# One argument to the tile framework: the order of a decoder layer's instructions is laid down against its time-line model

## Chip, cores and metric

The kernel runs on one core of a Trainium2 chip. The metric is the device time of one execution in microseconds (us); the table further down gives the median of three runs.

## What is computed

One decoder layer for a prompt of 1024 tokens and eight sample sequences of 8 tokens each, which share all weights. The reference, cut to what matters:

```python
def decoder_layer(x, c, lp, attend, s0_re, s0_im):
    mod = jax.nn.silu(c) @ lp['ada_w'] + lp['ada_b']
    sh1, sc1, g1, sh2, sc2, g2, sh3, sc3, g3 = jnp.split(mod, ADA_CHUNKS, axis=-1)
    h = x + 0.5 * g1[:, None, :] * swiglu(rms_modulate(x, lp['norm_ffn1'], sh1, sc1),
                                          lp['ffn1_w_in'], lp['ffn1_w_out'])
    mix, k, v, sr, si = token_mixer(rms_modulate(h, lp['norm_mix'], sh2, sc2), lp, attend, s0_re, s0_im)
    h = h + g2[:, None, :] * mix
    h = h + 0.5 * g3[:, None, :] * swiglu(rms_modulate(h, lp['norm_ffn2'], sh3, sc3),
                                          lp['ffn2_w_in'], lp['ffn2_w_out'])
    return h, k, v, sr, si

def token_mixer(u, lp, attend, s0_re, s0_im):
    q, k, v, xs, ga, gb = jnp.split(u @ lp['w_in'], IN_SPLITS, axis=-1)
    o_a = attend(q, k, v, lp['sb_bias'])          # stick-breaking attention, 8 heads of 64
    y, sr, si = s5_ssm(xs, ...)                   # 32 groups, one complex state of 64 each
    zg = jax.nn.gelu(y)
    o_b = zg * jax.nn.sigmoid(zg @ lp['glu_w'] + lp['glu_b'])
    merged = jax.nn.sigmoid(ga) * (o_a @ lp['w_branch_a']) + jax.nn.sigmoid(gb) * (o_b @ lp['w_branch_b'])
    return merged @ lp['w_out'], k, v, sr, si
```

The width is 1024, the inner width of the two feed-forward nets 2816. All tensors are float32; the kernel multiplies in pairs of 16-bit parts (three products for one).

## The kernel before, in words

Activations lie transposed: 128 partitions by 8 slices of the model width, with 1092 columns (1024 prompt tokens, 64 sample tokens, 4 of padding), which are worked in three chunks of 364 or two halves of 546. The program is straight-line: Python loops are unrolled while it is traced, and there is no branch on the device.

Its stages follow each other: the first feed-forward net (`ffn`, up to 755 us of the profile), with the projection of the conditioning (`ada_steps`) and the tables of the state-space model (`ssm_params`, `ssm_prep`) traced into it; the combined input projection and the state-space run (`mixer_a`, `ssm_run`); the gated unit (`glu`); attention of prompt and samples with the rest of the projection as side work (`attend_prompt`, `attend_sample`, the list `gates`); the merge of the two branches and the output projection (`mixer_b`); the second `ffn`; the final norm.

Weights come through the class `Weights`: `fetch` issues a DMA on SyncE's queue into one of two buffers `wf` (L122), `measure` takes their largest magnitude on VectorE (L89), GpSimd spreads it over the partitions (L82), and `split` cuts them into two 16-bit parts, the high one on ScalarE (L101), the low one on VectorE (L102). In the feed-forward nets, `seven_products` (from L468) computes one block of 128 inner channels with seven products of 24 matmuls each, in three PSUM tiles X, Y and Z that are added to more than once. Its last VectorE reads are L503 (of Y, after the product `s3`), L506 and L510. Product `a22` writes to Y again, and so waits for L503:

```python
    add(Y, "s3", "t3", False)
    v.tensor_add(c22, view(Y), c22)
    tick()
    add(Z, "s4", "b22", False)
    ...
    add(Y, "a22", "t4", False)
```

Who sets the order: the kernel only traces instructions. When the block `tile.TileContext` closes, the framework's scheduler lays down one list for each engine and each DMA queue. It plays the program against a model of the machine. Each time an engine can take an instruction, it takes the one that was traced first among those that are ready at that moment of the model. On the chip each list then runs strictly in the order laid down, and an instruction whose input is late holds back all that stand behind it. By default the model is the framework's plain simulator; its choices are thus those of a moment that the plain simulator reckoned. Two kinds of edges bind the scheduler whatever the model is: `tc.issue_after(ins)` (the block's instructions on that engine stand behind `ins`) and `tc.keep_in_program_order`. Which buffer of a pool a tile gets is decided in the same pass.

## Time and profile before

| what | value |
|---|---|
| median of 3 runs | 2384.77 us |
| lowest, highest | 2381.21 us, 2393.02 us |
| the profiled execution's own time | 2397.24 us |
| its span, first to last instruction | 2395.5 us |
| TensorE busy | 2287.6 us (95%), 18391 matmuls |
| VectorE busy | 1678.2 us (70%) |
| ScalarE busy | 969.2 us (40%) |
| mean granted clock of TensorE | 0.982 of full |

The span is the time of all five engines together; busy is the time in which an engine had an instruction in work. TensorE's busy time is modelled at the ends of its matmuls, since they are pipelined. The granted clock is the share of full speed (2.4 GHz) at which TensorE could run; half of it is 1.2 GHz.

### The profile page before, as it was taken

What the parts mean: (1) busy time and instruction counts of PE and PEld (TensorE: products, weight loads), DVE (VectorE), ACT (ScalarE), POOL (GpSimd) and SP (SyncE); (2) the same over time, 40 slices, a digit from 0 to 9 for tenths busy, and PEclk for the clock granted to TensorE, in tenths of its full rate; (3) what the DMA queues carried; (4) which work ended last, traced back from release to release, by engine and by line L of the source; (5) the groups of instructions that cost most, each with busy time, mean ns of one, the idle gap of its engine ahead of it and who ended that gap; (6) DMA issues with size and microseconds to landing.
All of it is one profiled execution on the core that took longest, in us unless ns stands there. A gap on an engine that the chain in (4) does not pass through costs nothing.

```text
span 2395.5 us, 42875 instructions
## 1 busy us (share of the span) xinstructions
PE 2287.6 (95%) x18391; PEld 1626.9 (68%) x18391; DVE 1678.2 (70%) x3026; ACT 969.2 (40%) x1244; POOL 141.8 (6%) x193
## 2 busy tenths in 40 slices
PE   5999999999999999899999997999999999999997
PEld 2677778777787666685544452655688878888884
DVE  5966698886797626446788787697677655777735
ACT  3533331233331521245788787324443321333403
POOL 0000000000000000001133300000000000000000
PEclk8999999999999999989999998999999999999999
DMA  8133334433333144445244323522111143111302
GB/s 308 55 119 108 108 120 140 152 108 123 135 145 126 54 146 146 110 158 185 75 137 136 109 67 128 187 77 84 61 52 55 34 139 111 63 54 54 129 19 76
DMA packets 94191, 262.83 MB, mean 110 GB/s; under 512 B 13152, under 2 KB 50400, under 8 KB 83760
## 3 DMA queue, kind: packets, MB, share of 16 engines
q1 hardware_dynamic: 83632, 240.23, 29.3%
q0 software_dynamic: 5312, 17.34, 2.5%
q10 hardware_dynamic: 5056, 2.52, 0.5%
q8 instruction: 144, 2.36, 0.4%
q14 instruction: 47, 0.39, 0.1%
HBM read 204.10 MB, written 49.66 MB: 106 GB/s over the span
## 4 chain that ended last, share of the span: by engine, by line
PE 54%; DVE 13%; ACT 7%; DMA 5%; issue 3%; POOL 1%; SPq 1%; another core or an unknown queue 0%; ACTq 0%; DVEq 0%; POOLq 0%
PE u L481 19%; PE u L242 13%; PE u L226 11%; PE u L216 2%; PE z L1368 2%; DVE wl L102 2%; DVE mx L89 2%; DMA wf<-in_ffn_w_in 2%; ACT ae L1098 1%; DMA wf<-in_w_in 1%; PE z L226 1%; PE z L994 1%; PE o L1112 1%; DMA aw<-in_ada_w 1%; ACT ae L1016 1%
## 5 line engine op out<-in xcount | busy, mean ns | idle before, releaser
L226 PE MATMUL u<-u,wh 128*128 128x364 f16 (+1 forms) x1632 | 391.6, 319 | 6.3 <-ACT u L398 4.3
L242 PE MATMUL u<-h,wh 128*128 128x272 f16 (+1 forms) x2304 | 366.2, 280 | 4.9 <-DVE h L102 4.9
L101 ACT ACTIVATE wh<-wf,sc 128x1024 f16<-128x1024 f32 (+2 forms) x130 | 183.2, 1410 | 371.4 <-PE u L242 179.8
L89 DVE TENSOR_REDUCE mx<-wf 128x1 f32<-128x1024 f32 (+2 forms) x136 | 211.1, 1575 | 145.3 <-DMA wf<-in_ffn_w_in 80.3
L481 PE MATMUL u<-u,wh 128*128 128x272 f16 (+1 forms) x1824 | 288.0, 279 | 1.7 <-DVE mx L89 1.3
L242 PEld LDWEIGHTS <-wh 128*128 128x128 f16 x2560 | 249.2, 97 | 59.3 <-issue 6.9
L481 PEld LDWEIGHTS <-wh 128*128 128x128 f16 x2432 | 234.6, 98 | 66.3 <-issue 19.7
L226 PE MATMUL u<-u,wl 128*128 128x364 f16 (+1 forms) x816 | 260.2, 319 | 1.1 <-DVE wl L102 1.1
L102 DVE SCALAR_TENSOR_TENSOR wl<-wf,sc,wh 128x1024 f16<-128x1024 f32 (+2 forms) x130 | 209.2, 1609 | 73.3 <-ACT wh L101 72.8
L226 PEld LDWEIGHTS <-wh 128*128 128x128 f16 x1824 | 176.4, 98 | 114.7 <-issue 15.0
L242 PE MATMUL u<-h,wl 128*128 128x274 f16 (+1 forms) x1152 | 228.3, 280 | 0.0
L481 PEld LDWEIGHTS <-w3h 128*128 128x128 f16 x1824 | 175.7, 97 | 43.6 <-issue 7.4
L481 PE MATMUL u<-fac,w3h 128*128 128x272 f16 x1216 | 192.7, 279 | 0.0
L481 PE MATMUL u<-u,wl 128*128 128x272 f16 (+1 forms) x912 | 179.7, 278 | 0.0
L82 POOL PARTITION_ALL_REDUCE am<-mx x106 | 53.8, 514 | 1871.3 <-DVE mx L89 1834.1
L242 PEld LDWEIGHTS <-wl 128*128 128x128 f16 x1280 | 124.3, 97 | 26.9
L481 PEld LDWEIGHTS <-wl 128*128 128x128 f16 x1216 | 118.1, 97 | 26.2 <-issue 0.4
L226 PEld LDWEIGHTS <-wl 128*128 128x128 f16 x912 | 89.3, 98 | 58.3 <-issue 4.6
L481 PE MATMUL u<-fac,w3l 128*128 128x272 f16 x608 | 120.1, 279 | 0.0
L226 PEld LDWEIGHTS <-aside 128*128 128x128 f16 x864 | 83.0, 97 | 50.5 <-issue 1.7
L507 ACT ACTIVATE h<-h,iv 128x546 f32<-128x546 f32 x38 | 28.5, 749 | 206.8 <-DVE h L506 206.8
L481 PE MATMUL u<-fac,wh 128*128 128x272 f16 x608 | 97.9, 284 | 4.0 <-DVE st L523 4.0
(431 smaller groups left out, 3857.7 us busy)
## 6 DMA issues: line engine op xcount, KB each, us to landing
wf<-in_ffn_w_in SPq DMA_DIRECT2D x44, 1024.0 KB
aw<-in_ada_w SPq DMA_DIRECT2D x72, 512.0 KB
wf<-in_w_in SPq DMA_DIRECT2D x16, 1024.0 KB
wf<-in_ffn_w_out_a SPq DMA_DIRECT2D x16, 640.0 KB
xd<-xr SPq DMA_DIRECT2D x16, 546.0 KB
x<-xd SPq DMA_DIRECT2D x16, 546.0 KB
xd<-x SPq DMA_DIRECT2D x6, 1456.0 KB
sg<-gd SPq DMA_DIRECT2D x16, 546.0 KB
```

Of the source, the lines that this page charges most:

```text
L82: k.nc.gpsimd.partition_all_reduce(r, m, P, ABSMAX)
L89: k.nc.vector.tensor_reduce(m, src, axis=axis, op=ALU.max, apply_absolute_value=True)
L101: r = k.nc.scalar.activation(hi, src, AF.Copy, scale=s)
L102: k.nc.vector.scalar_tensor_tensor(lo, src, s, hi, op0=ALU.mult, op1=ALU.subtract)
L216: k.nc.tensor.matmul(ps[:, c, :n], wt[:, cols], act(kt, part)[:, c * CH:c * CH + n], start=kt == 0 and j == 0, stop=kt == nk - 1 and j == 2)
L226: k.nc.tensor.matmul(ps[:, :n], wt[:, cols], act(kt, part)[:, c * CH:c * CH + n], start=kt == 0 and j == 0, stop=kt == nk - 1 and j == 2)
L242: k.nc.tensor.matmul(ps[:, a:b], wt[:, cols], act(kt, part)[:, a0 + a:a0 + b], start=kt == 0 and j == 0, stop=kt == nk - 1 and j == 2)
L481: nc.tensor.matmul(t[:, c0:c1], wt[:, kt * P:kt * P + P], act(kt, part)[:, c0 - 240:c1 - 240], start=first and kt == 0 and j == 0, stop=kt ...
L507: nc.scalar.activation(h2, h2, AF.Silu, scale=iv)
L994: nc.tensor.matmul(p[:, q, :], ca[rows, ri, ga, 1:, :].rearrange("p a b -> p (a b)"), x[rows, ga, :], start=False, stop=ri == 1)
L1016: nc.scalar.activation(e, e, AF.Exp, scale=-1.0)
L1368: nc.tensor.matmul(ps[:M, :256], u[:, kt, part, tt * P:tt * P + M], wt, start=kt == 0 and j == 0, stop=kt == KD - 1 and j == 2)
```

## The change

The context that traces and schedules the kernel gets one argument more. The instructions, their operands, the pools and the two kinds of edges are traced as before; the scheduler plays them against another model of the machine, the framework's time-line simulator, in which engines, their sequencers, queues and the clock of TensorE have time lines of their own. So what can differ is the order within each engine's and each queue's list, the buffer that a tile gets, and the waits that follow from these. The whole diff:

```diff
-    with tile.TileContext(nc) as tc:
+    with tile.TileContext(nc, schedule_with_timeline_sim=True) as tc:
         trunk_kernel(tc, dr, out)
```

## Rows read from the trace of the kernel before

**Rows 1.** The page's first part: span and TensorE's busy time.

```profile
span 2395.5 us, 42875 instructions
PE 2287.6 (95%) x18391; PEld 1626.9 (68%) x18391; DVE 1678.2 (70%) x3026; ACT 969.2 (40%) x1244; POOL 141.8 (6%) x193
```

**Rows 2.** Windows by stage: length, busy us of PE, PEld, DVE, ACT, POOL; clock.

```profile
0.00:60.00 60.00, 33.68 (x400) 16.07 (x401) 32.52 (x74) 21.52 (x30) 1.80 (x9) 0.89 0.82 309
...
300.00:460.00 160.00, 152.62 (x1322) 121.93 (x1320) 138.12 (x479) 35.78 (x39) 5.26 (x11) 0.97 0.41 139
...
900.00:1032.00 132.00, 120.15 (x796) 83.57 (x793) 70.54 (x186) 25.47 (x41) 4.08 (x7) 0.92 0.45 126
...
1112.00:1484.00 372.00, 338.67 (x2322) 172.42 (x2321) 298.63 (x392) 298.78 (x438) 85.50 (x78) 0.97 0.38 118
1484.00:1682.00 198.00, 191.57 (x1377) 118.43 (x1375) 152.62 (x241) 74.16 (x71) 7.14 (x12) 0.99 0.34 119
1682.00:2330.00 648.00, 643.74 (x5388) 523.40 (x5387) 426.14 (x631) 211.90 (x243) 16.49 (x34) 1.00 0.20 69
2330.00:2395.50 65.50, 51.03 (x475) 31.23 (x473) 34.27 (x83) 21.82 (x33) 0.00 (x0) 0.91 0.20 69
```

**Rows 3.** TensorE's waits, 60:900 and 900:1110: total us, times, longest.

```profile
PE u L481 <- DVE st L523: 4.0, 1, 4.0
...
PE z L992 <- DMA ca<-ca: 7.2, 1, 7.2
```

**Rows 4.** Windows of the stretches around those waits and of attention's end.

```profile
440.00:450.00 10.00, 6.51 (x60) 4.42 (x64) 9.86 (x28) 2.19 (x2) 0.00 (x0) 0.66 0.14 57
...
1020.00:1030.00 10.00, 10.00 (x38) 7.75 (x37) 1.28 (x1) 2.75 (x4) 0.00 (x0) 0.50 0.13 34
1030.00:1040.00 10.00, 10.00 (x66) 8.18 (x67) 1.28 (x2) 0.79 (x2) 0.00 (x0) 0.72 0.89 215
...
1436.00:1484.00 48.00, 31.05 (x121) 9.95 (x121) 39.55 (x41) 40.41 (x53) 0.54 (x1) 0.88 0.37 135
```

**Rows 5.** Time line of TensorE around the wait of 7.2 us.

```profile
1011.45 0.27 PE L1368 MATMUL z<-wl,u 128*128 128x256 f16 x1
1018.92 2.15 PE L992 MATMUL z<-u,m 128*128 128x136 f32 x8 [7.20 <-DMA ca<-ca]
...
1032.00 0.61 PE L1368 MATMUL z<-wh,u 128*128 128x256 f16 x2
```

**Rows 6.** Time line of SyncE's DMA queue there.

```profile
1010.36 4.23 SPq L980 DMA_DIRECT2D m<-gp  x8
1014.72 0.37 SPq L982 DMA_DIRECT2D ca<-ca  x1
```

**Rows 7.** Time line of VectorE within one block of `seven_products`.

```profile
1777.73 2.35 DVE L89 TENSOR_REDUCE mx<-wf 128x1 f32<-128x1024 f32 x2 [2.21 <-DMA wf<-in_ffn_w_in]
1780.00 0.72 DVE L503 TENSOR_TENSOR q<-u,q 128x546 f32<-128x546 f32 x1
...
1786.38 1.28 DVE L102 SCALAR_TENSOR_TENSOR wl<-wf,sc,wh 128x1024 f16<-128x1024 f32 x1
```

**Rows 8.** Time line of TensorE in the same block: first matmuls of `s4` and `a22`.

```profile
1778.44 0.63 PE L481 MATMUL u<-u,w3h 128*128 128x272 f16 x4
...
1781.26 0.63 PE L481 MATMUL u<-u,wh 128*128 128x272 f16 x4
```

**Rows 9.** All instructions of line 503, with those that waited for them.

```profile
L503 DVE TENSOR_TENSOR q<-u,q x38: 704/717/721, 134.5 to 2233.5; 128x546 f32<-128x546 f32 x38
...
  PE u L481: 0.4, 1
```

**Rows 10.** ScalarE by line: one table load and the sigmoids of `mixer_b`.

```profile
L1501 ACT ACTIVATE sg<-sg 128x1092 f32<-128x1092 f32 x16 | 17.6, 1110 | 35.1 <-DMA sg<-gd 35.1
...
L1501 ACT ACT_TABLE_LOAD x1 | 1.3, 1283 | 4.4 <-DMA sg<-gd 4.4
```

## The prediction

> **What bounds the kernel now.** I read the shares of busy time first, then the windows by stage, then TensorE's waits, and last the time lines at the two longest waits and in one block of the feed-forward nets. The page's first part says that TensorE has work for 2287.6 of 2395.5 us [rows 1]. So no order of instructions can take away more than the 107.9 us in which it has none, plus what a low clock costs. The windows say where these are: 60 - 33.7 = 26.3 us in the first 60 us, 7.4 in 300 to 460, 11.9 in 900 to 1032, 33.3 in attention (1112 to 1484), 6.4 in 1484 to 1682, 4.3 in the 648 us of the second feed-forward net, 14.5 at the end [rows 2]. Start and end, 40.8 us together, are one chain each: the start waits for the first transfers (the DMA engines are 0.82 busy there [rows 2]), the end is the last chunk's norm behind the last product. What stands there has no side work to be put in, so I cost the change at nothing in both. The reader is to see that a reordering has 107.9 - 40.8 = 67.1 us of idle TensorE to play for, 63 of it outside the second feed-forward net.
>
> **What the change removes, adds and moves.** It adds no arithmetic. Each engine's busy time stays, but for a possible load of an activation table (below). It moves instructions within their lists, DMA issues on SyncE's queue too, so the cost is in waits: an instruction that the model took to be ready, and that on the chip is not, holds back what stands behind it. The trace of before has two such waits of TensorE that are plainly of this kind, and they give the price of one.
>
> The first is 7.2 us before L992, a matmul of the state-space run that needs the table `ca` [rows 3]. TensorE had been in the middle of the projection L1368, stopped after 1011.45, and took L1368 up again at 1032.00 [rows 5]: work that needed nothing of that table stood behind the late one. The transfer was issued only at 1014.72, behind eight others that take SyncE's queue 4.23 us to issue [rows 6]. The wait also costs clock. TensorE is granted 0.50 of full, that is 1.2 GHz, in the ten us after it and 0.72 in the next ten [rows 4], which is 10 x 0.50 + 10 x 0.28 = 7.8 us of full speed lost. Together 15.0 us. The second is 4.0 us before a product of the first feed-forward net, behind VectorE's L523 [rows 3]; the ten us around it have a clock of 0.66 [rows 4], so 3.4 us more, 7.4 together. VectorE is 9.86 of 10 us busy there: the small steps of `ssm_prep` were put in front of the one that frees the PSUM tile. The two are worth 22.4 us, one is worth 11.2 on the mean.
>
> How many there will be after the change, no row shows. From below: none, which gains 22.4. From above: I take one in each place where chains of small steps, their DMAs and the large products are merged. There are four: 300 to 460, 900 to 1032, 1112 to 1484 and 1484 to 1682 [rows 2]; the first feed-forward net's rest and the second net have one regular loop. At two in each the sum would be 8 x 11.2 - 22.4 = +67. I take one in each, because the two that are known stand in two of the four, so that one is the rate at which such places err. That is 4 x 11.2 = 44.8 against 22.4 paid now: +22.4 us.
>
> In the feed-forward blocks the cover is tight in one place only. Product `a22` starts at 1781.26 [rows 8] and waits for L503, which ends at 1780.00 + 0.72 = 1780.72 [rows 7], so 0.54 us are left. The measure of the next weights (L89, 2.35 us, itself behind a DMA for 2.21 us) stands in front of it already [rows 7]. All 38 blocks together made TensorE wait 0.4 us there [rows 9]. If the new order puts L503 first, nothing is gained, since TensorE doesn't wait. If it puts one cut of weights more in front (L102, 1.28 us [rows 7]) a block loses 1.28 - 0.54 = 0.74 us, with a second measure 2.35 - 0.54 = 1.81 us: 28 to 69 us over 38 blocks. I take zero, because the loop has the same readiness in each block and the row nearest is this order with its 0.54 us; the other end is a rival.
>
> Attention has 33.3 us of idle TensorE, 48 - 31.05 = 17.0 of it in the last 48 us, where the side work of `gates` is used up [rows 2, 4]. ScalarE works 298.8 and VectorE 298.6 us of 372 [rows 2], so both are four fifths full and no engine is the sole bound; the chain of one step goes through all three. In its last 48 us, without side work, ScalarE is 40.41 / 48 = 0.84 full [rows 4]; at that rate the stage would take 298.8 / 0.84 = 356 us, 16 less. From the other side a step that is put behind more side work loses what one wait costs, which the sum above has. I take zero beside it.
>
> So the sum is +22.4 us. It is made against the profiled execution (2397.24 us), which lies 12.5 above the median of the runs shown; the idle times and waits are no larger for that, so I carry the difference over: 2384.8 + 22.4 = 2407 us.
>
> **Rivals.** First, the order errs less (faster). If the time-line model has DMA issue and the small VectorE steps nearer to the chip, L1368 goes on while `ca` is on its way, and the add that frees the PSUM tile comes ahead of `ssm_prep`. That gives -22.4, and with attention at its end's rate -38: 2362 to 2346, and half the first gives 2374. For it: both waits are misjudged arrivals, which is what a truer model mends. Against it: the choice stays greedy by traced order, and no row shows what the other model takes for true. It decides where new waits number fewer than two.
>
> Second, no difference that counts: the regular loops, which hold most of the time, come out alike and waits merely change place. It gives 2385, with 12 us to either side, since about 0.5% is what a measurement of this kernel can tell from no change.
>
> Third, the feed-forward blocks lose their 0.54 us: +28 to +69 beside the waits, 2413 to 2476. For it: 38 repeats, and the measure stands in front of L503 even now. Against it: TensorE has a product of the next block that could go ahead meanwhile.
>
> Fourth, table loads. Now there is one load, 1.283 us, in front of the 16 sigmoids of L1501, which wait for their transfers [rows 10]; the exponentials of attention end before it. An order that puts sigmoids between the last exponentials costs ScalarE two loads each time. With 4 to 8 of them that is 10 to 21 us where ScalarE is 0.84 full [rows 4]: 2395 to 2406 alone. The Trainium skill, ScalarE: Activation LUTs, section What ACT_TABLE_LOAD costs, gives 2.66 us for a switch with its drain; by that estimate 4 to 8 sigmoids would cost 21 to 43 us. The trace agrees on the load itself (1283 ns), and no row shows the drain.
>
> **How the numbers follow.** The forecast has 0.36, with a range of its own from one to four extra waits, 2396 to 2430. Faster has 0.31, no difference 0.19, the blocks 0.10, the tables 0.04. So slower by over 0.5% has 0.36 + 0.10 + 0.04 = 0.50, within 0.5% 0.19, faster 0.31. Low end 2350: it takes in nearly all of the first rival. High end 2455: half of the third rival's reach is left out, as is the case of two waits in each place (2384.8 + 67 = 2452) just within. The predicted time is the forecast's.
>
> **What would show it.** In the profile after, the busy times of all engines should be those of before within 1%; if TensorE's differ, I misread the change. TensorE's waits should no longer name `ca` at L992 or L523 with several us; new waits of 3 us and more should appear in the four places, each with a granted clock below 0.8 right after it. The window 1682 to 2330 should still have TensorE busy for all but some 5 us; idle time there, with L503 or L510 as releaser, is the third rival. More than six table loads is the fourth. If idle TensorE in the middle falls below 50 us, the first rival holds and I am wrong in sign.

## The result and the profile after

| what | before | after |
|---|---|---|
| median of 4 runs each | 2386.89 us | 2424.5 us |
| lowest, highest | 2381.21, 2393.02 us | 2423.03, 2428.03 us |
| span of the profiled execution | 2395.5 us | 2422.7 us |
| mean granted clock of TensorE | 0.982 | 0.973 |

The ratio of the times is 1.0153, with a 95% interval of 1.0139 to 1.0168: slower by 1.5%. By the medians that is 37.6 us, by the two profiled executions 27.2 us, since the profiled execution of before lay some 10 us above its median. The account below is made between the two traces, and so explains the 27.2. One execution of all those behind this document, of the run with the late step further down, took 4716.89 us, twice as long as the six others of that run; it is left out of the ratio there.

The first part of the page of after, with the slices of TensorE's clock (in tenths, 40 slices of the span):

```profile
span 2422.7 us, 42961 instructions
PE 2296.3 (95%) x18391; PEld 1631.6 (67%) x18391; DVE 1670.9 (69%) x3026; ACT 975.7 (40%) x1244; POOL 134.9 (6%) x193
...
PEclk8999999999999999999999787999999999999998
```

Against [rows 1] the work is the same: as many matmuls, and TensorE, VectorE and ScalarE are busy within 1% of before (GpSimd, whose spans are rough, 5% less). The three low digits of the clock, slices 23 to 25, are the second half of attention.

To set stage against stage I cut both traces at the same events instead of at the same times: the first residual add of `ffn` (L579), the first matmul of L1368, the last sigmoid of `glu` (L1446) and the last output matmul of attention (L1112). Before, cut so (columns as in [rows 2]):

```profile
900.00:1006.30 106.30, 101.65 (x699) 68.35 (x697) 64.12 (x170) 20.18 (x31) 3.36 (x6) 0.98 0.45 130
1006.30:1100.30 94.00, 86.80 (x639) 69.12 (x639) 43.87 (x61) 40.05 (x53) 1.76 (x4) 0.89 0.50 152
1100.30:1482.80 382.50, 349.17 (x2399) 179.81 (x2399) 306.36 (x402) 301.01 (x442) 86.05 (x79) 0.97 0.38 119
```

After, cut at the same events, with four further stretches:

```profile
300.00:460.00 160.00, 156.85 (x1371) 124.78 (x1369) 134.00 (x465) 36.44 (x40) 6.51 (x11) 1.00 0.43 145
...
755.90:900.00 144.10, 136.03 (x1054) 85.83 (x1054) 84.74 (x207) 48.84 (x69) 11.26 (x12) 0.98 0.39 116
...
1004.90:1085.60 80.70, 80.70 (x646) 64.59 (x644) 43.91 (x55) 41.86 (x52) 1.75 (x5) 1.00 0.48 158
1085.60:1519.60 434.00, 368.61 (x2393) 186.79 (x2393) 307.78 (x399) 304.89 (x442) 78.59 (x78) 0.90 0.34 106
1519.60:1720.00 200.40, 195.88 (x1389) 121.66 (x1386) 145.91 (x226) 73.34 (x70) 5.28 (x12) 0.98 0.34 116
1720.00:2356.00 636.00, 636.00 (x5368) 519.51 (x5367) 427.72 (x643) 212.99 (x245) 14.84 (x34) 1.00 0.20 70
```

Attention takes 434.0 us instead of 382.5: +51.5. Up to its start (the last sigmoid) 1085.6 instead of 1100.3 us have gone by, -14.7, of which 13.3 lie between the first L1368 and the last sigmoid (80.7 instead of 94.0, at a clock of 1.00 instead of 0.89, TensorE never idle). Behind it 903.1 instead of 912.7 us follow, -9.6; the second feed-forward net has no idle TensorE left (636.00 of 636.00). So the new order is 24.3 us better everywhere else and 51.5 worse in attention, and 51.5 - 24.3 = 27.2. Of the 51.5 us, 32.1 are idle TensorE (434.0 - 368.6 = 65.4 against 382.5 - 349.2 = 33.3), and 19.4 are the same matmuls keeping it busy for longer (368.61 against 349.17 us), at a mean granted clock of 0.90 instead of 0.97.

What happens inside attention is seen in stretches of 20 us. After:

```profile
1160.00:1180.00 20.00, 20.00 (x153) 11.45 (x151) 12.75 (x15) 16.02 (x22) 3.68 (x4) 1.00 0.18 55
1180.00:1200.00 20.00, 20.00 (x147) 11.52 (x146) 9.96 (x14) 6.79 (x12) 4.62 (x6) 1.00 0.52 169
...
1420.00:1440.00 20.00, 15.03 (x97) 5.37 (x96) 18.90 (x17) 16.39 (x19) 0.00 (x0) 0.67 0.34 79
1440.00:1460.00 20.00, 15.02 (x79) 6.94 (x78) 15.58 (x22) 17.38 (x28) 0.00 (x0) 0.84 0.00 1
```

At first TensorE is full and VectorE and ScalarE have long pauses; later those two are 78 to 95% full and TensorE is idle for a quarter, at a lowered clock. The cause shows when only the side work, the gate projections of L226, is counted. After, the whole of attention and its two parts (TensorE and its weight loads alone, of this line):

```profile
1085.60:1519.60 434.00, 166.06 (x996) 94.99 (x994) 0.90 0.34 106
1085.60:1311.70 226.10, 166.06 (x996) 94.99 (x994) 0.99 0.37 121
1311.70:1519.60 207.90, 0.00 (x0) 0.00 (x0) 0.80 0.30 88
```

The same line before, in two halves:

```profile
1100.30:1291.00 190.70, 109.24 (x604) 57.05 (x602) 0.99 0.42 128
1291.00:1482.80 191.80, 74.00 (x394) 36.65 (x392) 0.96 0.34 110
```

The traces have 996 matmuls of side work in this stage after, and 998 before. A step of prompt attention ends with four matmuls L1112, so the steps can be counted. Before, the side work lasts until 1435.8 us, when 40 of the 48 steps are done, in 173 runs of 5.8 on the mean; after, it is used up at 1311.7, when 17 steps are done, in 75 runs of 13.3. That was the first theory: the side work comes too densely, so attention is held up while TensorE is full, and then runs bare. Cut where the side work ends, the stage looks like this, first after, then before:

```profile
1085.60:1311.70 226.10, 221.81 (x1546) 129.57 (x1545) 144.36 (x198) 142.31 (x215) 43.09 (x44) 0.99 0.37 121
1311.70:1519.60 207.90, 146.80 (x847) 57.23 (x848) 163.42 (x202) 162.57 (x229) 35.50 (x34) 0.80 0.30 88
...
1100.30:1435.80 335.50, 319.32 (x2281) 169.99 (x2280) 266.61 (x362) 260.46 (x391) 85.51 (x78) 0.98 0.38 116
1435.80:1482.80 47.00, 29.85 (x118) 9.82 (x119) 39.75 (x41) 40.54 (x53) 0.54 (x1) 0.89 0.38 138
```

While there is side work, TensorE is idle for 4.3 us after and 16.2 before. A bare step leaves it idle for about 2 us in either order (61.1 us in 31 steps, 17.2 in 8), and after there are 23 more of them. The runs below ask whether the density is all there is to it.

### The profile page after: what moved, and what is told of

It is laid out like the page before. It is cut to its first block, busy times and chain, and to the rows that moved or that the text cites. A ratio compares the mean times of both kernels' runs of the same rounds, so it can differ in the third digit from the quotient of the medians.

```text
span 2422.7 us, 42961 instructions
## 1 busy us (share of the span) xinstructions
PE 2296.3 (95%) x18391; PEld 1631.6 (67%) x18391; DVE 1670.9 (69%) x3026; ACT 975.7 (40%) x1244; POOL 134.9 (6%) x193
## 4 chain that ended last, share of the span: by engine, by line
PE 80%; DVE 7%; ACT 6%; DMA 5%; issue 1%; SPq 0%; POOL 0%; DVEq 0%; ACTq 0%; POOLq 0%
PE u L481 29%; PE u L226 19%; PE u L242 16%; PE u L216 5%; PE z L1368 2%; DMA wf<-in_ffn_w_in 1%; ACT ae L1098 1%; PE s L292 1%; PE o L1112 1%; PE z L226 1%; PE z L994 1%; DMA wf<-in_ffn_w_out_a 1%; DMA aw<-in_ada_w 1%; ACT ae L1016 1%; DVE wl L102 1%
## 5 line engine op out<-in xcount | busy, mean ns | idle before, releaser
L226 PE MATMUL u<-u,wh 128*128 128x364 f16 (+1 forms) x1632 | 384.3, 319 | 10.7 <-ACT u L398 6.2
L226 PE MATMUL u<-u,wl 128*128 128x364 f16 (+1 forms) x816 | 260.4, 319 | 0.0
L226 PEld LDWEIGHTS <-wh 128*128 128x128 f16 x1824 | 176.5, 98 | 118.3 <-issue 13.2
L82 POOL PARTITION_ALL_REDUCE am<-mx x106 | 51.5, 492 | 1932.5 <-DVE mx L89 1816.2
L226 PEld LDWEIGHTS <-wl 128*128 128x128 f16 x912 | 89.3, 98 | 57.3 <-issue 6.4
L226 PEld LDWEIGHTS <-aside 128*128 128x128 f16 x864 | 83.0, 97 | 50.1 <-issue 1.2
L481 PEld LDWEIGHTS <-w3l 128*128 128x128 f16 x912 | 88.4, 97 | 19.0
```

Source lines behind the costliest of these rows:

```text
L82: k.nc.gpsimd.partition_all_reduce(r, m, P, ABSMAX)
L226: k.nc.tensor.matmul(ps[:, :n], wt[:, cols], act(kt, part)[:, c * CH:c * CH + n], start=kt == 0 and j == 0, stop=kt == nk - 1 and j == 2)
L481: nc.tensor.matmul(t[:, c0:c1], wt[:, kt * P:kt * P + P], act(kt, part)[:, c0 - 240:c1 - 240], start=first and kt == 0 and j == 0, stop=kt ...
```

## Experiments

All ratios are to runs of the kernel before on the same chip (medians of 2388 to 2399 us); a stage is the time from the last sigmoid of `glu` to the last output matmul of attention.

**Side work released evenly (two runs).** Each gate projection is traced six steps late, and may be issued only after the end of the step six before its place; once with the new order, once with the default.

```diff
...
-        while n_gates - len(gates) < (n_gates - 3) * done / steps:
-            gates.pop(0)()
+        ends.append(k.step_end)
+        while gates and n_gates - len(gates) < (done - 6) / 3.7:
+            with tc.issue_after(ends[done - 1 - 6]):
+                gates.pop(0)()
```

> The changed kernel, with the side work of attention spread: each of the thirteen projections left in the list of gates is traced six steps late and its instructions on TensorE are queued behind the end of the step six before, so that they are spread over all 48 steps and stay the less urgent work. Theory A (attention's loss is the place of the side work: the new order uses it up in the first two fifths and then has none): the stage from the last sigmoid of the gated unit to the last product of attention, 434 us in the changed kernel, comes back to 375 to 395, and the kernel to 2424 - 45 = 2379 us (2365 to 2392). Theory B (the new order of attention's own instructions on ScalarE and VectorE is worse, whatever the side work does): the stage stays at 420 or more and the kernel at 2410 or more.

> The same edges in the kernel before, with the default order. Theory A: its side work lasted for five sixths of attention already, so what can be gained is the last 48 us, where TensorE had 17 us idle: 382 us become 365 to 385, the kernel 2365 to 2390. Theory B says nothing of the side work: 2387 plus or minus 6.

Measured: 2454.37 us, ratio 1.0242 (1.0214 to 1.027), with the new order, and 2445.63, 1.0198 (1.0173 to 1.0224), with the default. The stage took 453.1 and 408.4 us. So even release made both slower. Theory A fell in both runs; theory B gave the numbers of the first (420 us or more, 2410 or more), but the second, which it left at 2387, came out 2% slower. In the new order two holes are plain in TensorE's waits (total us, times, longest): at the start, where no side work was free yet, and right behind the stage, where the merge waited for its input:

```profile
PE z L1091 <- ACT az L1100: 15.8, 1, 15.8
...
PE u L216 <- DMA ob<-od: 12.9, 1, 12.9
```

Only the first lies within the stage. By subtraction it would take 453.1 - 15.8 = 437.3 us without that hole, no less than in the new order, so holes alone don't explain it.

**Even release without the holes.** Each third of a projection (24 matmuls) gets its own release, ten steps ahead of an even spread, so that the start has work and the end is free.

```diff
...
-        unit_chunks(k, cur["w"], slice(q * P, q * P + P), act, KD, f)
+        for c in range(3):
+            with k.pace():
+                unit_chunk(k, cur["w"], slice(q * P, q * P + P), act, KD, c, f)
...
+    def pace():
+        e = int(1.25 * len(chunks)) - 10
+        chunks.append(e)
+        return tc.issue_after(ends[min(e, len(ends) - 1)]) if e >= 0 else ExitStack()
...
```

> The new order, but a third of each gate projection (24 matmuls) may go only after a certain step of attention, ten steps ahead of an even spread (one third per 1.25 steps). So side work stays available at the start, lasts until step 38 of 46, and ends before attention does; the run with even release without that lead had holes at both ends. Theory A, density (the new order puts three times as much side work into each wait of attention as that wait lasts, so attention is slowed while TensorE is full, and then ends alone): the attention stage falls from 434 to 380 to 400 us, and with the 24 us won elsewhere the time is 2360 to 2390 us, below the new order by 35 to 60 and not above the kernel before. Theory B, grain (the matmuls of side work stand in runs of 12 on the mean instead of 5, whichever step they go to): the stage stays above 420 us and the time above 2410.

Measured: 2442.08 us, ratio 1.0174 (1.0142 to 1.0205). The stage took 455.1 us, although the side work now lasted until step 38 (in the kernel before: 40). Theory A fell, so density is not the whole of it; the numbers are those of theory B, grain, and the side work did stand in runs of 12 on the mean. The waits between the engines grew: VectorE's in that stage begin, in the even release (total us, times, longest), with

```profile
DVE az L1030 <- PE P L1028: 38.0, 20, 5.5
DVE az L1208 <- ACT ae L1207: 17.9, 5, 4.9
DVE az L1102 <- ACT ae L1098: 16.8, 10, 5.2
```

where the kernel before has 14.2, 9.5 and 5.4 us (the same waits, one line number lower for the second).

**All side work ahead of attention (two runs).** The list `gates` is emptied before `attend_prompt` begins, so the two costs stand one after the other.

```diff
+    for f in gates:
+        f()
     for _ in attend_prompt(k, qT, kT, vt, range(4), scales):
         done += 1
-        while n_gates - len(gates) < (n_gates - 3) * done / steps:
-            gates.pop(0)()
...
-    for f in gates:
-        f()
```

> The changed kernel with all thirteen projections traced ahead of attention: no side work in it at all, so that attention's chain stands alone. The projections take 1008 matmuls x 0.154 us = 155 us, attention without side work went at about 0.30 to 0.33 percent per us in both kernels, so 300 to 330 us. Theory A: the stage takes 440 to 490 us in this kernel and in its twin of the kernel before, the same within 12 us, and this kernel stays the faster by the 24 us that the new order gained outside attention. Theory B: the stage is longer here than in the twin by 30 us or more, and this kernel is not the faster one.

> The twin of the run before it: the kernel before with all thirteen projections traced ahead of attention, default order. Theory A: a stage of 440 to 490 us against 382 with the side work inside, so 2387 + 60 to 105 = 2447 to 2492 us; the loss of the change is seen here without the change, by the place of the side work alone. Theory B: the stage is 400 us or less, since this order of attention's own instructions is the good one, and the kernel stays below 2410.

Measured: 2486.5 us, ratio 1.0368 (1.0332 to 1.0405), with the new order, and 2532.0, 1.0558 (1.0524 to 1.0592), with the default: 45 us apart, where 24 were expected. Windows of the new order: side work with attention's preparation, then attention alone, from its first output matmul to its last.

```profile
1092.00:1250.50 158.50, 153.71 (x996) 96.84 (x993) 47.43 (x62) 45.53 (x64) 13.61 (x19) 0.99 0.35 123
1250.50:1590.70 340.20, 240.26 (x1383) 98.22 (x1385) 259.44 (x336) 259.49 (x377) 66.36 (x59) 0.78 0.27 77
```

And of the default order:

```profile
1261.20:1617.80 356.60, 246.97 (x1384) 98.05 (x1385) 262.00 (x336) 262.66 (x379) 63.66 (x60) 0.78 0.26 73
```

Alone, attention takes 340.2 us in the new order and 356.6 in the default: laid down without side work, the new order of attention's own instructions is the faster one, and the second theory stated for these runs, that it is the slower, fell. With the side work ahead the stage takes 501.0 and 512.7 us, within 12 us of each other as the first theory says, but above its 440 to 490. So what the two orders hide by merging is 501.0 - 434.0 = 67.0 us in the new one and 512.7 - 382.5 = 130.2 in the default, of side work that takes 161 and 156 us alone. The loss is in the merging. A rough estimate from these numbers fits the density reading: 17 steps at 340.2 / 48 = 7.1 us are 120 us, with 161 of side work 281, and they were done in 226; 31 bare steps give 220, and 207.9 were seen.

**The default order made as dense.** The score matmuls of a step stand behind the projections that the new order has ahead of it (by TensorE's lists, in twelfths of attention, 292, 169, 256, 183, 36 side matmuls; in the new order 305, 162, 304, 95, 142).

```diff
...
+                            with tc.issue_after(k.side) if k.side else ExitStack():
+                                nc.tensor.matmul(ps[:, :n], ks[:, h, P * j:P * j + P], qs[:, h, i, cols], start=i == 0,
+                                                 stop=True, skip_group_check=True)
...
-        while n_gates - len(gates) < (n_gates - 3) * done / steps:
+        while gates and len(ends) < done / 1.35:
             gates.pop(0)()
+            ends.append(k.end)
+        if len(ends) > 0:
+            k.side = ends[min(len(ends), int(done / 1.35) + 1) - 1 - 0] if gates else None
...
```

> The default order, but the score matmuls of an attention step stand behind the gate projections that the new order has put ahead of that step (one whole projection per 1.35 steps), so side work lies as densely as in the new order and is used up at step 17 of 46; all else stays with the default. Theory A, density: the attention stage goes from 382.5 to 425 to 445 us, the time to 2430 to 2450. Theory B, the loss lies in how the new order arranges attention's own instructions and not in the side work: the stage stays within 10 us and the time at 2380 to 2400.

Measured: 2503.88 us, ratio 1.0444 (1.0414 to 1.0474), the stage 482.0 us. Density forced in this way costs, as theory A says, but about twice what it gave: 99.5 us instead of 42 to 62. Forced places can cost something of their own (the even release in the default order had cost 408.4 - 382.5 = 25.9 us), and this run does not tell the two apart.

**Whole lists carried over (five runs).** What remained was to leave each model everything but attention. The two kernels trace the same instructions, so the sequence in which one kernel's list holds them can be laid on the other as issue-order edges:

```diff
+def lay_order(tc, nc):
+    traced = nc.cur_bb.bb.instructions
+    for engine, text in ORDER.items():
+        own = [i for i in traced if str(i.engine) == "EngineType." + engine]
...
+        for a, b in zip(row, row[1:]):
+            tc.add_manual_dep(b, a.name, mybir.DependencyInfo(mybir.DependencyClass.NoSync,
+                                                              mybir.DependencyReason.DATA), reason="issue_after")
...
```

`ORDER` holds, for each engine named, the places of attention's instructions in the other kernel's list. The runs differ in the engines in it, and in the direction.

> The new order everywhere, except that the 1976 matmuls from the first score matmul of attention to its last output matmul stand on TensorE in the sequence of the kernel before (an issue-order edge from each to the next); VectorE, ScalarE, GpSimd and SyncE stay with the new order. Theory A (TensorE's list in attention is the loss: side work stands in runs that do not fit the waits of the chip, 13.4 matmuls on the mean instead of 5.4 and used up at step 17 instead of 40): the attention stage falls from 434 to 380 to 395 us, and the time to 2365 to 2390, below the kernel before because the 24 us outside attention stay won. Theory B (the loss lies in the order on ScalarE and VectorE, which the uneven TensorE list merely follows): the stage stays above 415 us and the time above 2405.

> As the run before it, and in attention the 432 instructions of ScalarE, 382 of VectorE, 75 of GpSimd and 78 of SyncE stand in the sequence of the kernel before too. Theory A: nothing is added by this, the time lies within 8 us of the run with TensorE's list alone, 2362 to 2390. Theory B: only here does the stage fall to 380 to 390 us and the time to 2360 to 2375. If both runs stay above 2400, what is gained outside attention hangs together with what is lost in it.

> The default order everywhere, except that the 2096 matmuls of attention's window stand on TensorE in the sequence of the new order. Theory A: the stage goes from 382.5 to 425 to 445 us and the time to 2430 to 2450, more than the new kernel because the 24 us outside attention are not won. Theory B: the stage stays below 400 us and the time below 2405.

> The counterpart of the run with TensorE's list alone: the new order, but in attention ScalarE (432 instructions), VectorE (382), GpSimd (75) and SyncE (78) stand in the sequence of the kernel before, and TensorE stays with the new order. Since the evacuations of the gate projections are among ScalarE's, the side work is now spread to step 38 by the scheduler itself, in runs of 14.2 matmuls on the mean. Theory C (the lists of the engines fit only as a set, and each taken alone loses): the stage stays at 415 to 455 us, the time at 2400 to 2450. Theory D (ScalarE's and VectorE's lists alone carry the loss, and TensorE's follows them): the stage falls to 380 to 395 us and the time to 2362 to 2385.

> The default order, but in attention all five lists stand in the sequence of the new order. If attention is the whole loss and what is won outside it is independent of that: the stage goes from 382.5 to 430 to 442 us, the time to 2432 to 2452, some 24 above the new kernel. If the two hang together: below 2425.

| model outside attention | lists in attention | stage, us | median, us | ratio (95%) |
|---|---|---|---|---|
| default | default (the kernel before) | 382.5 | 2386.89 | 1 |
| new | new (the kernel after) | 434.0 | 2424.5 | 1.0153 (1.0139 to 1.0168) |
| new | TensorE's of before, others replanned | 451.9 | 2447.19 | 1.019 (1.0156 to 1.0223) |
| new | the other engines' of before, TensorE's replanned | 446.8 | 2436.91 | 1.0206 (1.0189 to 1.0223) |
| new | all of before | 388.6 | 2371.88 | 0.9882 (0.9854 to 0.9911) |
| default | TensorE's of after, others replanned | 454.5 | 2470.15 | 1.029 (1.0259 to 1.0322) |
| default | all of after | 431.7 | 2452.77 | 1.0274 (1.0257 to 1.0291) |

Three things follow. First, attention is the whole loss and the rest is independent of it: with all of before's lists the stage falls back to 388.6, with all of after's lists it rises to 431.7 in the other kernel. The version with all lists of before is 1.2% faster than the kernel before and faster than the kernel after, because it keeps what the new order wins elsewhere. Second, neither TensorE's list nor those of the others carry the loss alone. TensorE's own list of before, with its 172 short runs, gave 451.9 us, more than the kernel after: theory A of the first of these runs fell, and with it the grain of the side work as the whole cause. TensorE's list of after in the default order took 454.5 us and 2470.15, above both ranges of its theory A. Theory D of the run with the other four lists fell as well, and its theory C held (446.8 us, 2436.91). The lists fit as a set. The expectation that the stage falls only with all lists came true, but not the reason given for it, that ScalarE's and VectorE's lists carry the loss. Third, there are two ways to lose, and the traces tell them apart by where TensorE is idle:

| lists in attention | steps with side work: us, TensorE idle | bare steps: us, TensorE idle |
|---|---|---|
| the kernel before | 40: 335.5, 16.2 | 8: 47.0, 17.2 |
| new, all of before | 40: 337.9, 18.5 | 8: 50.7, 18.3 |
| the kernel after | 17: 226.1, 4.3 | 31: 207.9, 61.1 |
| default, all of after | 17: 224.3, 3.1 | 31: 207.4, 63.4 |
| new, TensorE's of before | 40: 402.3, 64.0 | 8: 49.6, 19.6 |
| new, the other engines' of before | 38: 383.9, 54.2 | 10: 62.9, 24.0 |
| new, even release without the holes | 38: 397.8, 57.9 | 10: 57.3, 21.1 |

A bare step costs some 2 us of idle TensorE whichever lists it comes from, and dense side work, which is what the change brings, leaves 31 of them instead of 8. The partial repairs have few bare steps, but 54 to 64 us of idle TensorE in the steps with side work, where the lists were cut for different moments. That the density alone, and no other trait of the new lists, makes the 51.5 us is not shown by a run of its own: the dense versions have stages of 431.7 us and more, and the sparse ones lie anywhere between 382.5 and 455.1.

The time of the last run, 64.8 us above the median of before on the same chip, lies just above the 2432 to 2452 expected, the stage within its 430 to 442. The stage is 49.2 us longer; by the spans of the traces, 2449.2 against 2395.5, the whole is 53.7 longer, and the trace of before lay above its median.

The second way is seen in VectorE's waits in attention. TensorE's list of before alone, others replanned:

```profile
DVE az L1207 <- ACT ae L1206: 29.3, 6, 10.7
DVE az L1030 <- PE P L1028: 23.9, 17, 5.3
DVE ae L1018 <- ACT ae L1017: 23.4, 22, 2.6
```

All lists of before:

```profile
DVE az L1030 <- PE P L1028: 16.8, 23, 1.9
DVE az L1207 <- ACT ae L1206: 8.6, 4, 4.0
...
DVE ae L1018 <- ACT ae L1017: 5.0, 9, 0.9
```

With one order of TensorE, the VectorE instructions of a sample step (L1207) wait up to 10.7 us for ScalarE, and hold back the prompt steps behind them; with the matching lists of all engines the first and the last of these three waits shrink to a third or less, and the middle one from 23.9 to 16.8 us.

**The price of one misplaced wait.** In the default order the last output step of the state-space run is traced four column tiles later in L1368, so that its table `ca` has landed.

```diff
-    steps = [(), (0, 0, 1), (1, 1, 2), (0,), (2, 2, 3), (1,), (3,), (2, 3), (), (), (), (3,)]
+    steps = [(), (0, 0, 1), (1, 1, 2), (0,), (2, 2, 3), (1,), (3,), (2, 3), (), (), (), (), (), (), (), (3,)]
```

> The default order with the last output step of the state-space run traced four column tiles later in the projection L1368, so that its matmuls L992 come 96 matmuls later in the list and the table ca has landed by then. If the prediction's price of one misplaced wait is right (7.2 us of wait and 7.8 us of low clock), the time falls by 12 to 17 us against the kernel before. If the clock lost after the wait is not paid in time, it falls by 6 to 8 us. If the later step only shifts a wait to the gated unit behind it, it stays within 4 us.

Measured: 2388.77 us, ratio 0.9953 (0.9932 to 0.9974), which is 11 us (6 to 16). The wait is gone, and the clock stays full where [rows 4] had 0.50 and 0.72:

```profile
1010.00:1020.00 10.00, 10.00 (x94) 8.96 (x92) 1.41 (x10) 2.05 (x5) 0.00 (x0) 1.00 0.70 142
1020.00:1030.00 10.00, 10.00 (x70) 8.09 (x67) 1.88 (x2) 3.71 (x6) 0.00 (x0) 1.00 0.22 73
1030.00:1040.00 10.00, 10.00 (x85) 8.55 (x84) 0.68 (x2) 1.64 (x4) 0.00 (x0) 1.00 0.88 224
```

L1368 takes 1007.6 to 1063.6 instead of 1006.3 to 1075.9 us, 13.6 less, which is more than the 7.2 us of the wait: the clock that follows a wait is paid in time, as the prediction had it. Part of it is lost again behind L1368, where the gated unit now waits for its input (TensorE's waits: total us, times, longest):

```profile
PE u L226 <- ACT z L101: 1.9, 1, 1.9
...
PE u L226 <- DVE z L102: 1.4, 2, 1.1
```

From the first L1368 to the last sigmoid 9.5 us are won (84.5 against 94.0), so the third expectation, a wait moved into the gated unit, came true in part. The time won, 11, lies one below the 12 to 17 expected; its interval takes in much of that range and the 6 to 8 of a clock that costs nothing too, so it is the trace that decides, and not the time.

## Why the prediction was right or wrong

**The time and the sign** were right: 2424.5 us against 2407, within the range, slower by more than 0.5%. The reasons were not, and that the time came out is luck. Outside attention the sum has 3 x 11.2 - 22.4 = +11.2 us, and the traces have -24.3; in attention it has one wait, +11.2, and the traces have +51.5. The two misses, -35.5 and +40.3, cancel but for 4.8 us.

**Start and end at nothing**: right. TensorE is idle for 28.6 us in the first 60 (before 26.3) and for 14.5 at the end, as before.

**No arithmetic, busy times within 1%**: right, but for GpSimd (134.9 against 141.8 us).

**The two waits of before go away**: right. No wait of TensorE is left between 900 and 1085 us, and 440 to 450 runs at full clock. SyncE's queue of after shows why L992 no longer waits (columns as in [rows 6]):

```profile
979.03 1.38 SPq L980 DMA_DIRECT2D m<-gp  x3
980.46 0.43 SPq L982 DMA_DIRECT2D ca<-ca  x1
```

The table is asked for at 980.46 us, and the group that needs it begins at 1010; before, it was asked for at 1014.72, after TensorE had stopped [rows 5, 6]. The price of 15.0 us for this wait was nearly right too: the late step alone gave 13.6 in L1368 (9.5 up to the last sigmoid), and the new order 13.3 between the first L1368 and the last sigmoid. The price of the second wait, 7.4 us, no run tried alone; ahead of L1368 the new order won 1.4 us in all.

**One such wait in each of four places, +22.4 in sum**: this step failed. Outside attention, start and end, the new order made waits of over 3 us at three instructions only, two of them in the stretch 755.9 to 900, which I had not named, and one in the merge (TensorE's waits of 60 to 900, then of 1520 to 1720):

```profile
PE z L946 <- DMA m<-m: 4.0, 1, 4.0
PE u L226 <- DVE tmp L410: 3.4, 1, 3.4
...
PE u L481 <- DVE q L503: 0.8, 1, 0.8
...
PE u L216 <- ACT mt L1500: 4.5, 1, 4.5
```

The stretch 300 to 460 has 3.15 us of idle TensorE instead of 7.4, and 900 to 1085 none. Outside attention the sum is -24.3, about the -22.4 of the first rival, though the shares differ (13.3 from L1368 on, 9.6 behind attention, 1.4 ahead of L1368). The rival's reason, a model with arrivals nearer to the chip's, fits the earlier transfer of `ca`; no run here shows what the model takes for true.

**Attention at zero beside the sum**: this step failed too, and it decided the sign: 51.5 us instead of one wait's 11.2. My lower bound came from ScalarE's rate where side work had run out, and the upper one from single waits. Neither looked at what keeps the stage short: in the kernel before 130 of 156 us of side work are hidden, spread over 40 of 48 steps. There was the risk: an order that puts the same side work in the first 17 steps hides 67 of 161. The loss shows as no single wait. The longest of TensorE's in that stage is 3.3 us; the view begins (total us, times, longest)

```profile
PE P L1107 <- DVE az L1030: 17.1, 17, 2.3
PE z L1091 <- ACT az L1100: 9.2, 7, 3.3
PE o L1112 <- ACT az L1032: 8.9, 10, 2.5
```

and the stage has 434.0 - 368.6 = 65.4 us of idle TensorE, where before had 33.3. The rival's gain of 16 us for attention had a true part: attention alone is 16.4 us shorter in the new order (340.2 against 356.6). It is lost in the merging.

**The feed-forward blocks at zero**: nearly right. Product `a22` waited for L503 0.8 us in all 38 blocks ([rows 9] had 0.4). The stretch with the second net's blocks lost its 4.3 us of idle time instead of growing. The third rival fell. Its range was added up unevenly: the high end, 2476, has the 22.4 us of the waits in it, the low end, 2413, has not.

**Table loads**: ScalarE's time line has six of them in either trace, each of 1.28 us, the one in front of the 16 sigmoids among them [rows 10]; where the prediction counts one load, it counts that one alone. The fourth rival fell.

**Idle time in the middle**: it did not fall below 50 us; it rose from 67.1 to 83.3, which is 126.4 (2422.7 - 2296.3) less 28.6 in the first 60 us and 14.5 in the last stretch. The part of the first rival that spoke of attention is thereby refuted.

**The carry-over**: I made the sum against the profiled execution and took its distance from the median as harmless. The medians differ by 37.6, the traces by 27.2. The difference is the spread of the kernel before, and no trace here explains it.

What stays open: why the new model puts more than twice as much side work into each step (996 matmuls in 17 steps against 998 in 40). TensorE's list shows that it does; no run here changed the model itself. Nor was the even distribution tried with every engine's list cut for it by the scheduler; the four-list run comes nearest (side work to step 38, but in runs of 14.2), and it lost.

## What to carry to other kernels

Ask of each stage not only which waits it has, but how much work it hides and where the filler is used up: here a denser merging in a stage whose chain is long and whose TensorE is full with filler cost 51.5 us, more than any single wait. When two schedules each win in a part, carry the better part over as a whole, the lists of all engines together; a part of the lists alone cost more than it brought in each of the three ways tried here.

## What the runs showed that was not expected

A bare chain pays twice. With no side work attention left TensorE idle for 340.2 - 240.3 = 99.9 us, and the granted clock fell to 0.78; in the kernel before, filled to 349.17 of 382.5 us, it was 0.97. And pinning a good list of one engine made things worse: the same 1976 matmuls in the same sequence took 388.6 us with the lists of the other engines that belong to it, and 451.9 with those laid down anew.
